# Transposed activations of a four-layer trunk: ACT reads a whole PSUM tile before DVE does

## The chip, the cores and the metric

The kernel runs on one core of one Trainium2 chip. The metric is the device time in microseconds (us) of one launch, as the median of several runs. PE is the matrix engine (TensorE), PEld its weight loads, DVE the vector engine, ACT the scalar engine, POOL is GpSimd and SP is SyncE, which here issues most DMAs.

## What is computed

A decoder trunk of four layers over 512 tokens of width 1024, in float32. Each layer normalises its input, mixes along the tokens with one of three mixers (S5, HGRN2, sliding-window attention, then S5 again), multiplies by a gate, projects back, normalises and adds:

```python
h = x
for i in range(DEPTH):                       # 4: S5, HGRN2, attention, S5
    u = rms_norm(h, norm_pre[i])
    if kind == 0:   y = s5_branch(u, ...)
    elif kind == 1: y = hgrn2_branch(u, ...)
    else:           y = swa_branch(u, ...)
    h = h + rms_norm(y, norm_post[i])
```

Each branch starts with a projection `u @ w_in` (1024 to between 2048 and 4096 columns). That first projection needs u with the channels on the partitions, so u is transposed.

## The kernel before

**Split products.** A float32 product is made of three matmuls on values that are rounded for the fast float32 path: every matrix is a high part and a low part (the rest). For the weights ACT copies the high part `whi` (w_conv, L182) and DVE subtracts for the low part `wlo` (L183). For the activations the high part is `xh`, the low part `xl`. In the weight-times-x loop (ws_steps, L228) each block of 128 channels k takes hi·xh, hi·xl and lo·xh in turn, so PE needs `xl` of a block one matmul after `xh` of it.

**From a layer to the next.** `out_proj` (L328) forms the output of layer L in PSUM tiles `ops` (L243) for four blocks of 128 tokens, tb 0 to 3. For each piece ACT squares it into `junk` for the sum of squares (L339) and DVE multiplies it by the gain into `yg` (L341). When a token block is complete, `finish` sums the two parts on DVE (`po_st`, L345), POOL raises to the power -1/2 (`rstd`, L253 and L254, giving `rs_r`), and DVE adds to the residual `h` (L350). `norm_stats` then prepares the next layer's input: ACT squares h (L274), POOL makes the factor, DVE scales (`xs`, L277). `spill` writes h to memory from SP (L356).

**The transposes.** `norm_xt` (L279 to L299) is called for token blocks (0, 1) together, for (2,) and for (3,). PE transposes blocks of xs into a PSUM tile `xtp` (L292). A tile has `per` slices, one slice per channel block k. For tokens (0, 1) it has two slices of 256 tokens, so there are four tiles; for (2,) and (3,) it has four slices of 128 tokens, so there are two tiles each. All these tiles, and some others of the mixers, share the tag "ca", of which there are two buffers: a third tile can be written only when the first has been read to its end. For every slice ACT scales and rounds it into `xh` (L296) and DVE forms scale times slice minus xh, which is `xl` (L298). The first layer has no low part of x there (`xl` is None); the three later entries do.

**Where they stand in the order.** The tiles of tokens (0, 1) are made inside the `out_proj` of the layer before, between the matmuls of token blocks 2 and 3. The tiles of (2,) and (3,) are made in the next layer's first projection (`first_blocks`, L301, for layers 1 and 2; the same pattern in `s5_rest` for layer 3, with the calls in its loop over half and b). There PE multiplies four blocks of output channels b by the first 256 tokens (half 0). Ahead of its fourth block PE transposes the two tiles of tb 2, named A and B here, then does the fourth block, then transposes the two tiles of tb 3, C and D here, and then starts half 1 (tokens 256 to 511), whose first matmul needs the first slice of C. C goes into A's buffer and D into B's.

```python
for half in range(2):
    for b in range(4):
        if half == 0 and b == 3:
            for _ in self.norm_xt(L, (2,)):       # tiles A, B
                pass
        self.ws(pss[b][...], w[b // 2], b % 2, self.x, half * 256, half * 256 + 256)
    if half == 0:
        for _ in self.norm_xt(L, (3,)):           # tiles C, D
            pass
```

In layers 1 and 2 the framework's scheduler puts the instructions of the engines in order, by its own estimates; layer 3 (L995ff) runs under a hand-written order for PE, DVE, ACT and SP, in which instructions stay as the code issues them. Beside the transposes, DVE and ACT have other work at each entry: in layer 1 the softmax of the lower bounds (`lb_e` and so on, L1060 to L1073, with one exp on ACT, L1062) and small tables of the later S5 layer (`lam`, `th`, `ap`, L404 to L479); in layer 2 the sine and cosine of the rotary embedding (L413 to L421, L1291); in layer 3 the S5 kernel tables (`q`, `vt`, `t`, L713 to L731), which wait for a parameter transfer `prm` (L706).

Of the kernel before, what the change touches and what calls it, by code (L numbers as in the profile page):

```python
# [20 lines left out]
KB = 8  # L21
# [87 lines left out]
class Trunk:  # L109
# [169 lines left out]
    def norm_xt(self, L, tbs):  # L279

        nc = self.nc
        xh, xl = self.x
        xs = self.xs
        n = len(tbs)
        c = slice(tbs[0] * 128, tbs[0] * 128 + 128 * n)
        per = 4 // n
        for k2 in range(KB // per):
            ps = self.psum.tile([P, per, 128 * n], F32, tag="ca", name="xtp", bufs=2)
            for kk in range(per):
                k = per * k2 + kk  # L290
                for i, tb in enumerate(tbs):
                    nc.tensor.transpose(ps[:, kk, i * 128:(i + 1) * 128], xs[:, tb, k * 128:(k + 1) * 128], self.ident)  # L292
            for kk in range(per):
                k = per * k2 + kk
                g = self.gpre[:, L * KB + k:L * KB + k + 1]
                nc.scalar.activation(out=xh[:, k, c], in_=ps[:, kk, :], func=AF.Copy, scale=g)  # L296
                if xl is not None:
                    nc.vector.scalar_tensor_tensor(out=xl[:, k, c], in0=ps[:, kk, :], scalar=g, in1=xh[:, k, c].bitcast(F32), op0=ALU.mult, op1=ALU.subtract)  # L298
            yield  # L299

# [1341 lines left out]
```

## Time and profile before

| | |
|---|---|
| median of 3 runs | 1119.49 us (1118.13 to 1121.62) |
| the profiled execution's own time | 1116.3 us |
| its span, first to last instruction | 1114.5 us |
| mean granted TensorE clock | 0.973 of full |
| PE, DVE, ACT, POOL busy | 93%, 67%, 45%, 9% of the span |
| chain that ended last | PE 63%, DVE 15%, ACT 6%, DMA 6%, issue 5% |

The profiled execution is 3.2 us below the median of the runs. Times of rows are microseconds from the start of the span. In a timeline a row is the start, the duration, the engine, line, operation, output <- inputs, shapes and count; in square brackets stands how long the engine was idle before and what ended the idle time. The second of two instructions of one engine often starts before the first has ended (by some tenths), so durations of neighbours can't be added; where that matters, the distance between starts is used. The granted clock of a stretch is a fraction of 2.4 GHz; at 0.50 PE runs at 1.2 GHz.

### The profile page before, as it was taken

What the parts mean: (1) busy time and instruction counts of PE and PEld (TensorE: products, weight loads), DVE (VectorE), ACT (ScalarE), POOL (GpSimd) and SP (SyncE); (2) the same over time, 40 slices, a digit from 0 to 9 for tenths busy, and PEclk for the clock granted to TensorE, in tenths of its full rate; (3) what the DMA queues carried; (4) which work ended last, traced back from release to release, by engine and by line L of the source; (5) the groups of instructions that cost most, each with busy time, mean ns of one, the idle gap of its engine ahead of it and who ended that gap; (6) DMA issues with size and microseconds to landing.
All of it is one profiled execution on the core that took longest, in us unless ns stands there. A gap on an engine that the chain in (4) does not pass through costs nothing.

```text
span 1114.5 us, 17031 instructions
## 1 busy us (share of the span) xinstructions
PE 1031.2 (93%) x6480; PEld 822.3 (74%) x6480; DVE 750.5 (67%) x1458; ACT 504.2 (45%) x933; POOL 103.2 (9%) x162
## 2 busy tenths in 40 slices
PE   5999975999999999999999898999997879988997
PEld 4755544778899798998978885666676767766876
DVE  6786759585698777887856565556664468863752
ACT  4344425554452314333244534688743355645540
POOL 2000000030200000000011022100002010100200
PEclk9999988999999999999999999999999889998999
DMA  6574233533432324414153452211125357544331
GB/s 230 137 190 126 74 85 98 171 114 126 143 103 81 114 71 132 144 65 151 61 189 124 122 145 62 74 57 53 61 95 167 117 155 238 173 124 146 104 103 57
DMA packets 70577, 133.31 MB, mean 120 GB/s; under 512 B 28896, under 2 KB 40032, under 8 KB 69472
## 3 DMA queue, kind: packets, MB, share of 16 engines
q1 hardware_dynamic: 65664, 119.04, 34.6%
q10 hardware_dynamic: 4832, 13.19, 3.6%
q8 instruction: 51, 0.84, 0.3%
q14 instruction: 30, 0.25, 0.1%
HBM read 100.51 MB, written 20.15 MB: 108 GB/s over the span
## 4 chain that ended last, share of the span: by engine, by line
PE 63%; DVE 15%; ACT 6%; DMA 6%; issue 5%; SPq 2%; POOL 1%; ACTq 1%; DVEq 0%; POOLq 0%
PE pj L228 26%; PE ops L243 13%; PE zps L243 4%; PE vps L243 3%; PE sps L1120 2%; PE scps L1328 2%; DVE wlo L183 2%; SPq L773 2%; ACT whi L182 2%; PE aops L1364 2%; DMA rsw<-rraw 1%; DMA prm<-in_s_bc 1%; PE ptp L1359 1%; DVE sg L1049 1%; PE yps L858 1%
## 5 line engine op out<-in xcount | busy, mean ns | idle before, releaser
L183 DVE TENSOR_TENSOR wlo<-wraw,whi 128x1024 fp32r<-128x1024 f32 x116 | 143.2, 1251 | 65.0 <-ACT whi L182 56.1
L228 PE MATMUL pj<-xh,whi 128*128 128x512 f32 (+1 forms) x496 | 182.3, 370 | 0.0
L228 PE MATMUL pj<-xl,whi 128*128 128x512 f32 (+1 forms) x496 | 177.9, 360 | 2.5 <-DVE xl L298 2.4
L228 PE MATMUL pj<-xh,wlo 128*128 128x512 f32 (+1 forms) x496 | 177.4, 359 | 0.0
L182 ACT ACTIVATE whi<-wraw 128x1024 fp32r<-128x1024 f32 x116 | 120.7, 1056 | 79.4 <-PE pj L228 38.2
L228 PE MATMUL pj<-xf,wraw 128*128 128x512 f32 (+1 forms) x320 | 116.0, 512 | 0.0
L228 PEld LDWEIGHTS pj<-xh,whi 128*128 128x128 f32 x496 | 96.3, 195 | 16.8 <-issue 5.8
L228 PEld LDWEIGHTS pj<-xl,whi 128*128 128x128 f32 x496 | 96.9, 196 | 14.6 <-DVE xl L298 3.2
L228 PEld LDWEIGHTS pj<-xh,wlo 128*128 128x128 f32 x496 | 96.5, 195 | 13.6 <-issue 1.7
L243 PE MATMUL ops<-whi,gh 128*128 128x512 f32 x256 | 101.6, 398 | 2.7 <-ACT gh L1051 2.2
L243 PE MATMUL ops<-wlo,gh 128*128 128x512 f32 x256 | 100.7, 394 | 1.1 <-DVE wlo L183 1.0
L243 PE MATMUL ops<-whi,gl 128*128 128x512 f32 x256 | 100.5, 395 | 0.0
L228 PEld LDWEIGHTS pj<-xf,wraw 128*128 128x128 f32 x320 | 59.2, 192 | 40.4 <-issue 36.7
L243 PEld LDWEIGHTS ops<-whi,gh 128*128 128x128 f32 x256 | 48.2, 188 | 13.8 <-ACT gh L1051 3.0
L243 PEld LDWEIGHTS ops<-wlo,gh 128*128 128x128 f32 x256 | 48.2, 188 | 13.2 <-DVE wlo L183 2.7
L243 PEld LDWEIGHTS ops<-whi,gl 128*128 128x128 f32 x256 | 48.1, 188 | 11.3 <-DVE gl L1052 0.9
L228 PE MATMUL pj<-yl,whi 128*128 128x512 f32 x128 | 51.0, 399 | 3.5 <-DVE yl L950 3.5
L228 PE MATMUL pj<-yh,whi 128*128 128x512 f32 x128 | 51.3, 401 | 0.5 <-ACT yh L946 0.5
L228 PE MATMUL pj<-yh,wlo 128*128 128x512 f32 x128 | 50.8, 397 | 0.0
L341 DVE TENSOR_TENSOR yg<-ops,gpost 128x512 f32<-128x512 f32 x32 | 21.9, 688 | 36.9 <-ACT junk L339 36.6
L243 PE MATMUL vps<-wlo,xh 128*128 128x256 f32 x160 | 45.3, 283 | 0.0
L243 PE MATMUL vps<-whi,xl 128*128 128x256 f32 x160 | 45.3, 283 | 0.0
(279 smaller groups left out, 2106.4 us busy)
## 6 DMA issues: line engine op xcount, KB each, us to landing
wraw<-in_s_in SPq DMA_DIRECT2D x32, 512.0 KB, 6.3
wraw<-in_hg_in SPq DMA_DIRECT2D x32, 512.0 KB, 3.6
wraw<-in_at_in SPq DMA_DIRECT2D x20, 512.0 KB, 4.2
wraw<-in_s_glu SPq DMA_DIRECT2D x16, 512.0 KB, 3.8
wraw<-in_s_out SPq DMA_DIRECT2D x16, 512.0 KB, 3.5
hd<-h SPq DMA_DIRECT2D x6, 1024.0 KB, 4.0
prm<-in_s_bc SPq DMA_DIRECT2D x16, 256.0 KB, 4.6
ub<-ut SPq DMA_DIRECT2D x16, 256.0 KB, 4.2
```

What stands on the lines that cost most here:

```text
L182: nc.scalar.activation(out=hi, in_=raw, func=AF.Copy)
L183: nc.vector.tensor_tensor(out=lo, in0=raw, in1=hi.bitcast(F32), op=ALU.subtract)
L228: self.nc.tensor.matmul(ps, lhsT=l[k // 4][:, k % 4, c], rhs=r[:, k, n0:n1], start=k == 0 and n == 0, stop=k == KB - 1 and n == len(terms) ...
L243: self.nc.tensor.matmul(ps, lhsT=l[:, k, c], rhs=r[k // per][:, k % per, :], start=k == 0 and n == 0, stop=k == KB - 1 and n == 2)
L341: nc.vector.tensor_tensor(out=yg[:, tb, f], in0=ps, in1=gp[:, f], op=ALU.mult)
L773: nc.sync.dma_start(out=toep[128 - n:128, jj, :, :], in_=ksb[0:n].rearrange("p a g h -> p (a g) h"))
L858: nc.tensor.matmul(o, lhsT=u[:, g, :], rhs=d["toep"][:, :, g, :], start=True, stop=False)
L1049: nc.vector.tensor_tensor(out=sg, in0=sg, in1=y[:, k, :], op=ALU.mult)
L1120: nc.tensor.matmul(ps[:, c, :], lhsT=k[:, c * 128:c * 128 + 128], rhs=q4[:, c, :, 1, :], start=True, stop=True)
L1328: nc.tensor.matmul(ps[:, bb, lo:256], lhsT=self.q[r, 4 * p + 2 * b2 + bb, qs], rhs=self.k[r, p, ks], start=True, stop=True)
L1359: nc.tensor.transpose(tp[:, f, bb, :], sm[:, bb, f * 128:f * 128 + 128], self.ident)
L1364: nc.tensor.matmul(ops[64 * i:64 * i + 64].rearrange("p b q -> p (b q)"), lhsT=self.v[:, n - 1 + f, kv * 64:kv * 64 + 64], rhs=pts[i][:, f ...
```

## The change

In `norm_xt` the loop over the slices of a tile is split in two: ACT's reads of all slices come first, then DVE's reads of all slices. The same instructions run with the same operands, only the order in which they are issued is another.

```diff
             for kk in range(per):
                 k = per * k2 + kk
                 g = self.gpre[:, L * KB + k:L * KB + k + 1]
                 nc.scalar.activation(out=xh[:, k, c], in_=ps[:, kk, :], func=AF.Copy, scale=g)
-                if xl is not None:
+            if xl is not None:
+
+                for kk in range(per):
+                    k = per * k2 + kk
+                    g = self.gpre[:, L * KB + k:L * KB + k + 1]
                     nc.vector.scalar_tensor_tensor(out=xl[:, k, c], in0=ps[:, kk, :], scalar=g, in1=xh[:, k, c].bitcast(F32), op0=ALU.mult, op1=ALU.subtract)
             yield
```

Lines behind L299 are four lower down in the changed kernel (L339 becomes L343, and so on), and the xl line moves from L298 to L302.

**ACT at the entry of layer 1**, from the exp of the lower bounds on (tiles xtp_2454 and xtp_2467 are A and B). Before:

```order
L1062 ACTIVATE lb_e_2328<-lb_e_2328 128x32 [waits DVE_49]
L509 DMA lam_2765<-in_s5_lam 128x288 [waits DMAHW4_49,DMAHW0_49,Activation_49]
L296 ACTIVATE xh_2125<-xtp_2454,gpre_96 128x128 [waits PE_49]
L296 ACTIVATE xh_2125<-xtp_2467,gpre_96 128x128 [waits PE_49]
L296 ACTIVATE xh_2125<-xtp_2454,gpre_96 128x128 [waits DVE_49]
L296 ACTIVATE xh_2125<-xtp_2467,gpre_96 128x128 [waits DVE_49]
L431 ACTIVATE lam_2765<-lam_2765 128x96 [waits DMAHW0_49]
```

and with the change:

```order
L1066 ACTIVATE lb_e_2328<-lb_e_2328 128x32 [waits DVE_49]
L513 DMA lam_2765<-in_s5_lam 128x288 [waits DMAHW4_49,DMAHW0_49,Activation_49]
L296 ACTIVATE xh_2125<-xtp_2454,gpre_96 128x128 [waits PE_49]
L296 ACTIVATE xh_2125<-xtp_2454,gpre_96 128x128 x3
L296 ACTIVATE xh_2125<-xtp_2467,gpre_96 128x128 [waits PE_49]
L296 ACTIVATE xh_2125<-xtp_2467,gpre_96 128x128 x3
L435 ACTIVATE lam_2765<-lam_2765 128x96 [waits DMAHW0_49]
```

Before, every read of ACT but a tile's first waits for DVE, and the two tiles take turns; now only the first of a tile waits, for PE, and the tiles come one after the other. The entries of layers 2 and 3 change in the same way.

**DVE in the out_proj of layer 0**, where the tiles of tokens (0, 1) for layer 1 are read (xtp_2249 and xtp_2288 are the third and fourth of them). Before:

```order
L341 TENSOR_TENSOR yg_1971<-ops_2215,gpost_1969 128x512 [waits Activation_49]
L298 SCALAR_TENSOR_TENSOR xl_2126<-xtp_2249,gpre_96,xh_2125 128x256 [waits Activation_49]
L345 TENSOR_REDUCE po_st_2261<-po_ss_1974 128x1
L350 SCALAR_TENSOR_TENSOR h_1747<-yg_1971,rs_r_2264,h_1747 128x1024 [waits DVE_49,Pool_49]
L298 SCALAR_TENSOR_TENSOR xl_2126<-xtp_2249,gpre_96,xh_2125 128x256 [waits Activation_49]
L277 TENSOR_SCALAR xs_2127<-h_1747,rs_r_2271 128x1024 [waits Activation_49,Pool_49]
L298 SCALAR_TENSOR_TENSOR xl_2126<-xtp_2288,gpre_96,xh_2125 128x256 [waits Activation_49] x2
L341 TENSOR_TENSOR yg_1971<-ops_2275,gpost_1969 128x512 [waits Activation_49]
```

and with the change:

```order
L345 TENSOR_TENSOR yg_1971<-ops_2215,gpost_1969 128x512 [waits Activation_49]
L349 TENSOR_REDUCE po_st_2261<-po_ss_1974 128x1
L302 SCALAR_TENSOR_TENSOR xl_2126<-xtp_2249,gpre_96,xh_2125 128x256 [waits PE_49,Activation_49]
L302 SCALAR_TENSOR_TENSOR xl_2126<-xtp_2249,gpre_96,xh_2125 128x256
L354 SCALAR_TENSOR_TENSOR h_1747<-yg_1971,rs_r_2264,h_1747 128x1024 [waits DVE_49,Pool_49]
L277 TENSOR_SCALAR xs_2127<-h_1747,rs_r_2271 128x1024 [waits Activation_49,Pool_49]
L302 SCALAR_TENSOR_TENSOR xl_2126<-xtp_2288,gpre_96,xh_2125 128x256 [waits PE_49,Activation_49]
L302 SCALAR_TENSOR_TENSOR xl_2126<-xtp_2288,gpre_96,xh_2125 128x256
L345 TENSOR_TENSOR yg_1971<-ops_2275,gpost_1969 128x512 [waits Activation_49]
```

`po_st` moves ahead of both low parts of the third tile, and both of them ahead of `h`; in the fourth tile the second low part no longer waits for ACT.

**DVE in layer 1 after the transposes**, around the first two `wlo` there (sin_2794 and cos_2795 are ACT's table values for the later S5 layer). Before:

```order
L446 TENSOR_TENSOR ap_2806<-mag_2791,cos_2795 128x64 [waits Activation_49]
L462 SCALAR_TENSOR_TENSOR u1_2842<-ap_2806,lam_2765 128x64 [waits DVE_49]
L404 TENSOR_TENSOR pw1_2873<-ap_2806 128x128
L464 TENSOR_TENSOR u1_2842<-u1_2842,u2_2843 128x64 [waits DVE_49]
L404 TENSOR_TENSOR pw2_2874<-ap_2806 128x128
L465 TENSOR_TENSOR co_2841<-u1_2842,den_2844 128x64 [waits DVE_49]
L467 TENSOR_TENSOR u2_2843<-ap_2806,lam_2765 128x64
L466 SCALAR_TENSOR_TENSOR u1_2842<-ap_2806,lam_2765 128x64 [waits DVE_49]
L472 TENSOR_SCALAR co_2841<-co_2841,cst_94 128x64
L468 TENSOR_TENSOR u1_2842<-u1_2842,u2_2843 128x64 [waits DVE_49]
L406 TENSOR_TENSOR ap_2806<-pw1_2873,pw2_2874 128x64
L183 TENSOR_TENSOR wlo_2367<-wraw_2362,whi_2366 128x1024 [waits PE_49,Activation_49]
```

and with the change:

```order
L467 TENSOR_TENSOR u2_2843<-ap_2806,lam_2765 128x64 [waits DVE_49]
L183 TENSOR_TENSOR wlo_2367<-wraw_2362,whi_2366 128x1024 [waits PE_49,Activation_49]
L183 TENSOR_TENSOR wlo_2371<-wraw_2364,whi_2370 128x1024 [waits DMAHW1_49,PE_49,Activation_49]
L450 TENSOR_TENSOR ap_2806<-mag_2791,cos_2795 128x64 [waits Activation_49]
L466 SCALAR_TENSOR_TENSOR u1_2842<-ap_2806,lam_2765 128x64 [waits DVE_49]
L408 TENSOR_TENSOR pw1_2873<-ap_2806 128x128
```

The eleven small table instructions that stood ahead of the first `wlo` now stand behind the second, since ACT's cosine for them has moved behind two weight copies and two evacuations.

## Rows read from the trace of the kernel before

**Rows 1.** The page's busy times: us, share of the span, instructions.
```profile
PE 1031.2 (93%) x6480; PEld 822.3 (74%) x6480; DVE 750.5 (67%) x1458; ACT 504.2 (45%) x933; POOL 103.2 (9%) x162
```
**Rows 2.** Waits by engine and releaser: us in total, times, longest us.
```profile
ACT xh L296 <- DVE xl L298: 23.8, 25, 3.6
...
PE xtp L292 <- DVE xl L298: 12.3, 4, 4.9
```
**Rows 3.** Timeline of ACT, out_proj of layer 0 and entry of layer 1.
```profile
292.69 0.47 ACT L296 ACTIVATE xh<-xtp,gpre 128x256 fp32r<-128x256 f32 x1 [1.76 <-DVE xl L298]
...
301.59 0.23 ACT L1062 ACTIVATE lb_e<-lb_e 128x32 f32<-128x32 f32 x1 [1.57 <-DVE lb_e L1061]
...
302.05 0.62 ACT L296 ACTIVATE xh<-xtp,gpre 128x128 fp32r<-128x128 f32 x2 [0.23 <-ACT lb_e L1062]
```
**Rows 4.** Timeline of DVE, the same stretch.
```profile
286.62 0.48 DVE L298 SCALAR_TENSOR_TENSOR xl<-xtp,gpre,xh 128x256 fp32r<-128x256 f32 x1
287.01 0.15 DVE L345 TENSOR_REDUCE po_st<-po_ss 128x1 f32<-128x2 f32 x1
...
292.17 0.48 DVE L298 SCALAR_TENSOR_TENSOR xl<-xtp,gpre,xh 128x256 fp32r<-128x256 f32 x1
...
293.77 0.69 DVE L341 TENSOR_TENSOR yg<-ops,gpost 128x512 f32<-128x512 f32 x1
...
303.05 0.60 DVE L298 SCALAR_TENSOR_TENSOR xl<-xtp,gpre,xh 128x128 fp32r<-128x128 f32 x2
...
306.40 0.21 DVE L436 TENSOR_TENSOR lrdt<-lam 128x64 f32<-128x64 f32 x1
...
307.80 0.25 DVE L298 SCALAR_TENSOR_TENSOR xl<-xtp,gpre,xh 128x128 fp32r<-128x128 f32 x1
```
**Rows 5.** Timeline of PE, entry of layer 1, and a wait later in that layer.
```profile
306.54 1.26 PE L292 MATMUL xtp<-cst,xs 128*128 128x128 f32 x8 [2.59 <-DVE xl L298]
...
308.68 0.41 PE L228 MATMUL pj<-xl,whi 128*128 128x256 f32 x1
...
336.23 1.05 PE L1107 MATMUL dps<-hq,hk 128*128 128x192 f32 x5 [1.00 <-DVE st L1110]
```
**Rows 6.** Windows: us, then busy of PE, PEld, DVE, ACT, POOL; PEclk, DMA, GB/s.
```profile
304.00:312.00 8.00, 5.46 (x32) 5.18 (x33) 6.70 (x31) 6.10 (x17) 0.00 (x0) 0.79 0.01 2
330.00:340.00 10.00, 8.99 (x70) 8.82 (x70) 9.83 (x42) 2.60 (x3) 0.00 (x0) 1.00 0.42 136
```
**Rows 7.** Timelines of ACT, DVE and PE, entry of layer 2.
```profile
619.72 0.61 ACT L296 ACTIVATE xh<-xtp,gpre 128x128 fp32r<-128x128 f32 x2
...
620.65 0.60 DVE L298 SCALAR_TENSOR_TENSOR xl<-xtp,gpre,xh 128x128 fp32r<-128x128 f32 x2
...
623.41 1.09 PE L292 MATMUL xtp<-cst,xs 128*128 128x128 f32 x8 [3.37 <-DVE xl L298]
...
625.23 0.42 PE L228 MATMUL pj<-xl,whi 128*128 128x256 f32 x1
```
**Rows 8.** Timelines of ACT, DVE and PE, entry of layer 3 and a later wait.
```profile
856.43 0.40 ACT L718 ACTIVATE c<-prm,cst 128x128 f32<-128x128 f32 x1 [4.58 <-DMA prm<-in_s_bc]
...
857.92 1.22 DVE L727 TENSOR_TENSOR vt<-ap,q 128x1024 f32<-128x1024 f32 x1
...
859.85 0.35 DVE L298 SCALAR_TENSOR_TENSOR xl<-xtp,gpre,xh 128x128 fp32r<-128x128 f32 x1 [0.43 <-ACT xh L296]
...
861.83 1.11 PE L292 MATMUL xtp<-cst,xs 128*128 128x128 f32 x4 [4.87 <-DVE xl L298]
...
864.30 1.22 DVE L730 TENSOR_TENSOR t<-ap,q 128x1024 f32<-128x1024 f32 x1
...
867.14 0.34 DVE L298 SCALAR_TENSOR_TENSOR xl<-xtp,gpre,xh 128x128 fp32r<-128x128 f32 x1
...
867.54 0.58 PE L228 MATMUL pj<-xl,whi 128*128 128x256 f32 x1 [1.76 <-DVE xl L298]
...
894.61 0.42 DVE L713 TENSOR_TENSOR q<-prm,co 128x256 f32<-128x256 f32 x1 [10.79 <-DMA prm<-in_s_bc]
```

## The prediction, made before the changed kernel had run

> **What bounds the kernel now.** I read the page's busy times first [rows 1]: PE is busy for 93% of the span, DVE for 67%, ACT for 45%. The end can only come earlier where PE stands still or runs slowly. The waits by engine and releaser come next [rows 2]: ACT's high parts waited 25 times for DVE's low parts, 23.8 us in all, and PE waited 12.3 us in four pieces to write a transposed tile, since the buffer was still being read by DVE. The first number is large and mostly worth nothing, as ACT has time. The second is PE's own idle time. Three of its four pieces stand in the timelines: 2.59 us at the entry of layer 1 [rows 5], 3.37 at layer 2 [rows 7], 4.87 at layer 3 [rows 8]; the fourth, 1.5, follows at layer 3. So the change is worth what it does at three entries, and at each I ask two things: when does DVE finish tiles A and B, which frees the buffers for C and D, and when does the first low part of C exist, which PE needs to go on.
>
> **Price of the pieces.** One low part takes 0.35 us [rows 8], two back to back 0.60 [rows 4, 7], so a further one costs 0.25 and four about 1.1. Two high parts take 0.62 [rows 3], so four also come to about 1.1. Turn by turn with nothing else between, one slice takes 0.35 plus a wait of 0.43 [rows 8], some 0.79, thus eight slices 6.3 us against about 2 × 1.1 us for DVE alone.
>
> **Term 1: the chain of statistics ahead of each entry, 1.2 us earlier.** In out_proj ACT's second read of the fourth tile of tokens (0, 1) waited 1.76 us for DVE [rows 3]. DVE's low part (start 292.17 [rows 4]) had stood behind xs, and ACT's junk, which must come before DVE's yg, stood behind that read. With the change ACT has both high parts done long before. DVE then runs two low parts and yg without a gap. Low part to next instruction is 0.39 (286.62 to 287.01 [rows 4]). Moreover po_st goes ahead of the third tile's low part, so that h, the squares and xs of token block 2 start 0.39 earlier, while both low parts run in the time that POOL takes for its power. So yg comes at 292.17 - 0.39 + 2 × 0.39 = 292.56 instead of 293.77 [rows 4]: 1.2 us. Everything behind it (h, the last squares, xs of block 3, and the small DMAs that ACT and SP issue after them) moves by this. The same pattern precedes layers 2 and 3, where ACT's longest wait is 3.6 [rows 2]. By itself it gives PE nothing, since the first transposes of an entry wait for no one; its worth lies in the next terms.
>
> **Term 2: layer 1, 2.8 us.** ACT's exp ended at about 301.8 [rows 3], now 300.6. High parts of A take until 301.8, of B until 302.9. DVE's lower bounds were done at 303.05, when its low parts started [rows 4]; now 301.85, and all highs of A are there. Low parts of A last until 303.0, of B until 304.1. PE's fourth block ended at 306.54 - 2.59 = 303.95 [rows 5], so the 2.59 are gone: C is transposed at once, D with a few tenths of a wait. What is late next is DVE. The order puts ten small table instructions ahead of C's low parts. Six such, a reciprocal among them, took from 306.40 to 307.80 [rows 4], so ten cost 1.9 to 2.3, from 304.1 to about 306.2. PE's matmul comes 0.4 after its low part starts (867.14 to 867.54 [rows 8]): 306.4 to 306.8 against 308.68 [rows 5]. That is 1.9 to 2.3. A second part is the clock: it was granted at 0.79 between 304 and 312, with PE busy for 5.46 us [rows 6], of which 0.21 × 5.46 = 1.1 us were lost. The wait that is left is about 1 to 1.5 us; one of 1.00 at 336.23 [rows 5] lies in a stretch with the clock at 1.00 [rows 6]. Bounds 1.9 and 3.4; I take 2.8, nearer that row.
>
> **Term 3: layer 2, 2.8 us.** High parts of A started at 619.72 and low parts at 620.65 [rows 7]; by term 1 ACT starts at 618.5 and is through with A at 619.65, and DVE, free at 619.45, does A's low parts until 620.9. ACT's cosine, which stood between the high parts, comes behind B. C is transposed at 620.95 instead of 623.41, its highs start at 621.6 and its first low part at 622.8, so PE goes on at 623.2 instead of 625.23 [rows 7]: 2.0. With a clock part like layer 1's 1.1 it is 3.1. I take 2.8.
>
> **Term 4: layer 3, 4.6 us.** Here the order is written by hand and the turns are strict. ACT's c waited for the parameter transfer until 856.43 [rows 8]; with term 1 that is 855.2. ACT's highs of A and B are then ready at 857.8, while DVE still does vt (857.92, 1.22 long, now from 856.72). A's low parts end at 859.05, B's at 860.15. C is transposed at 859.05 against 861.83, and t starts at 860.1 against 864.30. From t to the first low part of C there are 2.84 us (to 867.14), and 0.4 to PE's matmul: 863.3 against 867.54 [rows 8], 4.25 earlier. The next blocks no longer follow DVE and ACT's pitch of 0.79, which I put at 0.3. If the parameter transfer does not move, 3.4 is left.
>
> **Term 5: DVE in layer 1, charged 0.7.** Eleven table instructions that DVE did while ACT made weight copies now stand behind two wlo. One is 0.21 long [rows 4], so DVE stands idle for about 2.2 there and does this work later, in front of the heads. Bounds: 0, if PE has other matmuls to fill with, and 2.2. DVE is busy for 9.83 of 10 us later in the layer, but PE's wait in that stretch is only 1.00 [rows 5, 6]; I take a third.
>
> Nothing else changes: no instruction is added, each is as long as before, the DMAs stay in their order on SP and POOL. Work of ACT and DVE that moves earlier in tokens (0, 1) is under matmuls.
>
> **Sum.** 2.8 + 2.8 + 4.6 - 0.7 = 9.5. Against the profiled execution, 1116.3, that is 1106.8; the median of the runs is 3.2 higher, and on it the forecast is 1119.5 - 9.5 = **1110.0 us**. With the terms' bounds the gain lies between 1.9 + 2.0 + 3.4 - 2.2 = 5.1 and 3.4 + 3.1 + 4.6 = 11.1, 1114.4 to 1108.4. A median of three moves by another 1 to 2 (the runs went from 1118.1 to 1121.6), so I go down to 1106.
>
> **Rivals.** *Layer 3's gain is taken back at a parameter transfer.* DVE waited 10.79 us until 894.61 for a later prm [rows 8]. If that transfer is held by the weight loads ahead of it and not by PE's progress, what PE wins before is lost there, and 4.9 is left: 1114.6. For it: the wait is the longest of its kind in this stretch. Against: the loads ahead of it need buffers that PE frees, so it should move with PE. **0.20.**
>
> *Finer turns are better.* Reading a whole tile first makes its first low part come three high parts later, 3 × 0.25 = 0.75, at each tile for which PE waits with nothing else to do: C of each layer. In layers 1 and 2 both engines already had a second tile to work on while they waited, so there the total of their work is unchanged and only this cost remains. Layer 3 keeps the gain from its strict turns, about 3.1. Net 3.1 - 2 × 0.75 = 1.6: 1118.0, within the resolution. The Trainium skill ("Perfetto Trace Analysis", Optimizing Scalar/DVE Operations) speaks for this side: where the scalar and vector engines are not saturated but cause bubbles on others, breaking work into smaller pieces may let it finish sooner. By that rule turns are the finer pieces, and the engines are unsaturated here (45% and 67%); by the rows above the bubble comes from the end of a tile, not from its first slice. **0.12.**
>
> *Slower: DVE becomes the bound of layer 1's first heads.* The scheduler's new order leaves DVE idle for 2.2 us and puts up to 17 small instructions of 0.2, 3.4 in all, ahead of the heads' hk and hqt. If no matmuls of the projection are left to cover it, PE waits 5.6 for each of the first two head pairs, 11.2, in a stretch where DVE is already busy 98% [rows 6]. Layer 1's gain is lost with it: 11.2 - 2.8 - 4.6 = 3.8 slower, 1123.3. It decides from the point at which the wait of 1.00 at 336.23 [rows 5] grows beyond what the entries give. **0.05.**
>
> That the change does nothing is excluded: the order shows ACT's reads free of waits for DVE.
>
> **How the numbers follow.** A measurement of this kernel tells 0.3%, 3.4 us, from no change. The forecast's case has 0.63 and spans 1106 to 1114; with the first rival (1114.6, plus some run to run) the range is 1106.0 to 1116.5 and leaves out the other two, 0.17, and a little below. Both first cases are faster by over 3.4 us (below 1116.1): 0.83. The second rival is the same: 0.12. The third is slower: 0.05.
>
> **What would show it.** ACT's wait for DVE in the list of waits should nearly vanish, and PE's 12.3 us for xtp shrink to 3 to 4, most of it at layer 3. yg after the fourth tile should start about 1.2 earlier relative to its transposes. The clock around the entries of layers 1 and 2 should stay near 1. In layer 3, t should start about 4 us earlier relative to PE's last matmul of half 0. I am wrong if PE's low-part wait at C grows by what xtp's shrinks, if the DVE wait near the first heads of layer 1 grows to several us, or if the wait for prm at 894.61 grows by 4.

## The result, and the profile after

The changed kernel took 1108.03 us (median of 4 runs, 1105.03 to 1110.78) against 1119.28 (4 runs, 1118.13 to 1121.62): a ratio of 0.9896, 95% interval 0.9865 to 0.9927, 11.2 us less, where 9.5 were forecast. Run again later beside other kernels it took 1105.91 (6 runs) against 1119.78 (11 runs): 0.9871 (0.9841 to 0.9901).

The two profiled executions differ by less, 1110.78 against 1116.3 us, 5.5 us: the profile before came from an execution 3 us below the median of its kernel, the profile after from the slowest of its four. Where that comes from is shown below: a transfer landed late in layer 3, and the clock was lower behind it. The change is not the cause.

The page's first part after the change, as [rows 1]:

```profile
PE 1029.4 (93%) x6480; PEld 821.3 (74%) x6480; DVE 747.7 (67%) x1458; ACT 500.4 (45%) x933; POOL 103.9 (9%) x162
```

DVE and ACT are busy for about as long as before. Of the 5.5 us between the two spans 3.7 are idle time of PE (83.3 before, 79.6 after); the other 1.8 are busy time of PE (1031.2 and 1029.4), since the same matmuls run at a higher granted clock in some stretches. The waits by engine and releaser show the first part, beside [rows 2]:

```profile
ACT xh L296 <- PE xtp L292: 5.1, 6, 2.0
...
PE xtp L292 <- DVE xl L302: 4.4, 3, 3.1
...
PE pj L228 <- DVE xl L302: 3.2, 3, 1.9
```

ACT's high parts wait for PE's transposes now, and no wait of theirs for DVE is among the hundred largest. PE's wait to write a transposed tile is 4.4 instead of 12.3, a little above the forecast of 3 to 4; two waits at layer 3, 3.12 and 0.38, are most of it. PE's wait for low parts grew from 2.4 to 3.2, far less than the other shrank.

**Layer 1.** DVE's timeline after the change, as [rows 4]:

```profile
291.70 0.87 DVE L302 SCALAR_TENSOR_TENSOR xl<-xtp,gpre,xh 128x256 fp32r<-128x256 f32 x2
292.48 0.68 DVE L345 TENSOR_TENSOR yg<-ops,gpost 128x512 f32<-128x512 f32 x1
...
301.95 2.16 DVE L302 SCALAR_TENSOR_TENSOR xl<-xtp,gpre,xh 128x128 fp32r<-128x128 f32 x8
305.02 0.26 DVE L439 TENSOR_TENSOR th<-lam 128x96 f32<-128x96 f32 x1 [0.90 <-ACT lam L435]
...
306.77 2.06 DVE L302 SCALAR_TENSOR_TENSOR xl<-xtp,gpre,xh 128x128 fp32r<-128x128 f32 x8
```

yg comes at 292.48 instead of 293.77. PE was 0.09 ahead there, so the chain of statistics is 1.20 earlier: term 1 to the hundredth. The eight low parts of A and B take 2.16 us in one go. But the table instructions then start 0.9 late, since ACT's lam waited for its transfer. ACT and PE in the same stretch, as [rows 3, 5]:

```profile
300.78 2.18 ACT L296 ACTIVATE xh<-xtp,gpre 128x128 fp32r<-128x128 f32 x8 [0.23 <-PE xtp L292]
304.70 0.28 ACT L435 ACTIVATE lam<-lam 128x96 f32<-128x96 f32 x1 [1.75 <-DMA lam<-in_s_lam]
```

```profile
303.71 1.12 PE L292 MATMUL xtp<-cst,xs 128*128 128x128 f32 x8
305.29 0.74 PE L228 MATMUL pj<-xh,whi 128*128 128x256 f32 x4 [0.47 <-ACT xh L296]
307.08 0.38 PE L228 MATMUL pj<-xl,whi 128*128 128x256 f32 x1 [1.05 <-DVE xl L302]
```

C and D are transposed without a wait (2.59 before). PE's first low part of C is at 307.08 against 308.68, 1.5 earlier when the 0.09 are taken off. What is missing to the forecast's 1.9 to 2.3 is less than DVE's wait of 0.90 for lam. When the change was run again, lam had landed by 302.66, and PE's wait for the low part was 0.56 instead of 1.05.

**Layer 3.** DVE's timeline, as [rows 8]:

```profile
855.21 2.15 DVE L302 SCALAR_TENSOR_TENSOR xl<-xtp,gpre,xh 128x128 fp32r<-128x128 f32 x8
857.27 1.22 DVE L734 TENSOR_TENSOR t<-ap,q 128x1024 f32<-128x1024 f32 x1
...
859.67 2.15 DVE L302 SCALAR_TENSOR_TENSOR xl<-xtp,gpre,xh 128x128 fp32r<-128x128 f32 x8
```

Layer 3 began 2.68 us earlier in this execution. Taking that off, t starts 864.30 - 857.27 - 2.68 = 4.35 earlier (4.2 forecast), the first low part of C 867.14 - 859.67 - 2.68 = 4.8 (4.3 forecast).

### The profile page after: what moved, and what is told of

Its sections match the earlier page's. It is cut to its first block, busy times and chain, and to the rows that moved or that the text cites. A ratio compares the mean times of both kernels' runs of the same rounds, so it can differ in the third digit from the quotient of the medians.

```text
span 1109.0 us, 17044 instructions
## 1 busy us (share of the span) xinstructions
PE 1029.4 (93%) x6480; PEld 821.3 (74%) x6480; DVE 747.7 (67%) x1458; ACT 500.4 (45%) x933; POOL 103.9 (9%) x162
## 4 chain that ended last, share of the span: by engine, by line
PE 64%; DVE 13%; DMA 7%; ACT 6%; issue 5%; SPq 2%; POOL 1%; ACTq 1%; DVEq 0%; POOLq 0%
PE pj L228 26%; PE ops L243 14%; PE zps L243 4%; PE vps L243 3%; PE scps L1332 3%; PE sps L1124 2%; DVE wlo L183 2%; SPq L777 2%; PE aops L1368 2%; ACT whi L182 2%; DMA prm<-in_s_bc 1%; DMA rsw<-rraw 1%; PE yps L864 1%; PE ptp L1363 1%; PE yps L862 1%
```

## Stage by stage, over all the traces

Runs of one kernel scatter by 3 to 11 us, so that medians tell parts of 2 us apart only roughly. The traces do better for some stages: layer 1's rest, for example, lies between 239.7 and 239.8 us in seven of them. Others scatter in one and the same program, as layer 2's rest does (152.5 and 150.0 with the change). For each layer I took from PE's timeline the start of its first projection (the first matmul after the last `ops`), C's first low part, and the first `ops` of its own out_proj. **Entry** is from the first to 60 matmuls after the second, **rest** from there to the third. **Late** is one stretch of 120 matmuls in layer 3 (it starts at 973.7 in the trace before), and **prm** the time from SP's issue of the last parameter transfer to the DVE instruction q that reads it. All in us; bold where the layer has the whole reads.

| kernel (whole reads in) | L1 entry | L1 rest | L2 entry | L2 rest | L3 entry | late | prm |
|---|---|---|---|---|---|---|---|
| before (none) | 25.4 | 240.7 | 26.3 | 150.3 | 33.8 | 14.7 | 6.9 |
| layer 1 | **22.1** | **239.7** | 27.0 | 150.4 | 33.7 | 18.5 | 9.0 |
| layer 2 | 23.9 | 241.4 | **23.5** | **151.4** | 32.7 | 18.4 | 8.4 |
| layers 1, 2 | **22.9** | **239.8** | **24.7** | **150.9** | 33.5 | 15.2 | 7.3 |
| layer 3 | 24.9 | 242.2 | 26.2 | 152.3 | **28.0** | 18.4 | 8.1 |
| the change | **23.0** | **239.7** | **24.7** | **152.5** | **28.2** | 20.8 | 10.6 |
| the change again | **22.0** | **239.8** | **23.4** | **150.0** | **27.4** | 14.9 | 7.0 |
| out_proj tiles only | 23.7 | 241.3 | 23.7 | 149.7 | 31.2 | 19.1 | 9.0 |
| entry tiles only | 23.2 | 239.8 | 26.2 | 150.2 | 28.6 | 18.1 | 8.0 |
| C and D by turns | 21.6 | 242.1 | 22.9 | 150.4 | 27.7 | 18.6 | 8.9 |
| pairs | 22.6 | 239.7 | 23.0 | 150.2 | 29.1 | 19.3 | 9.5 |
| layer 2 pairs, else whole | **22.8** | **239.8** | 23.1 | 152.2 | **27.6** | 16.4 | 7.2 |

Means of bold against those of the kernels that read that whole layer by turns (the first, and the runs on other layers): layer 1's entry 22.6 against 24.7, its rest 239.8 against 241.4; layer 2's entry 24.0 against 26.5, its rest 151.2 against 151.0; layer 3's entry 27.8 against 33.4. In sum -2.2 - 1.7 - 2.5 + 0.2 - 5.7 = -11.8, beside -11.2 and -13.9 by the medians. Apart from late, a stage of one program differs by up to 2.5 us between two executions (layer 2's rest), so I take single parts as known to about 1 us, an estimate.

## The experiments

All edits but the last two, the pairs, are shown against the changed kernel and put the turns back where a condition holds; those of the pairs are shown against the kernel before.

**Out_proj tiles only, entry tiles only.** For the first:

```diff
                 nc.scalar.activation(out=xh[:, k, c], in_=ps[:, kk, :], func=AF.Copy, scale=g)
-            if xl is not None:
-
+                if xl is not None and n == 1:
+                    nc.vector.scalar_tensor_tensor(out=xl[:, k, c], in0=ps[:, kk, :], scalar=g, in1=xh[:, k, c].bitcast(F32), op0=ALU.mult, op1=ALU.subtract)
+            if xl is not None and not (n == 1):
                 for kk in range(per):
```

> Only the two-slice tiles of tokens (0, 1) are read whole; the four-slice tiles of the entries keep their turns. Theory of separate terms: yg after the fourth tile comes 1.2 us earlier relative to the transposes in all three out_projs, and each entry starts its low parts up to 1.2 earlier, less what small DMAs hold back: about 3 us in all, 1116.3 (1115 to 1118). Rival, the whole gain comes from the four-slice tiles and the earlier statistics are hidden: 1119.3 as before. Rival, the statistics chain is most of the gain: below 1113.

For the second the condition is the other one:

```diff
-                if xl is not None and n == 1:
+                if xl is not None and n == 2:
...
-            if xl is not None and not (n == 1):
+            if xl is not None and not (n == 2):
```

> Only the four-slice tiles at the entries of the layers are read whole; the out_proj keeps its turns. Theory of separate terms: what the whole change gives (11.2 us) without about 3 for the statistics chain: 1111 (1110 to 1113). Rival, the statistics chain is hidden: 1108 as with the whole change. Rival, the chain is most: above 1114.

Measured: 1110.96 us, ratio 0.9928 (0.9902 to 0.9954), and 1110.56, 0.9914 (0.9893 to 0.9936), against 1119.23. So they save 8.3 and 8.7 us alone and 11.2 together: the second agrees with the expectation, the first with its rival, and the parts overlap. The table says where. In layer 2 the out_proj tiles alone shorten the entry by 2.8 (23.7 against 26.5), more than the whole change, and the entry tiles alone by 0.3; in layer 3 they give 2.2 and 4.8 of the 5.7. I had counted an earlier start as at most 1.2 per entry, and that held: against the trace before, C's first low part with the out_proj tiles alone comes 0.85, 1.24 and 1.24 us earlier, counted from the start of layers 1, 2 and 3, which is 3.3 in all. What comes on top is PE's clock. In the 60 matmuls behind that low part it was granted at 1.00, 1.00 and 0.77, and before at 0.86, 0.82 and 0.64; they took 7.2, 7.2 and 7.8 us instead of 8.2, 8.6 and 9.2, another 3.6 in all. With the entry tiles alone it was 1.00, 0.81 and 0.77. How much of this the edit did is open, since the clock there differs in kernels that read an entry in the same way: with layer 1 read by turns, a wait of 2.46 at C's transposes left the 60 matmuls at 1.00 (run on layer 2 below), and one of 1.98 was followed by 0.83 (run on layer 3).

**By layer.** The condition was `L != 3`, `L == 3`, `L != 1` and `L != 2` in these four, for example:

```diff
-                if xl is not None and n == 1:
+                if xl is not None and L != 3:
...
-            if xl is not None and not (n == 1):
+            if xl is not None and not (L != 3):
```

> The change in layer 3's input alone (its out_proj tiles and its four-slice tiles). Theory of separate terms: 4.6 by the prediction, 5.7 by the shift of the matmuls between the two traces (1.0 in the out_proj, 4.65 at the entry): 1113.6 to 1114.7. Rival, a later parameter transfer takes it back: 1118 to 1119. Layers 1 and 2 should have stages as long as before within 0.3.

> The change in the inputs of layers 1 and 2 alone. Theory of separate terms: the complement of the run on layer 3, 11.2 - 5.7 = 5.5 at most; by the traces 3.3 in layer 1 and 1.6 at the entry of layer 2: 1114.4. Rival, layer 2 gives its part back at the rotary embedding's transfers, as the one profile of the changed kernel shows (2.2 lost after 1.6 won): 1116.5, with layer 2 as long as before or longer in this run's trace too.

> The change in layer 1's input alone. By the traces so far layer 1 (from its first projection to its out_proj) is 3.8 us shorter with the change: 1115.4. By the prediction's terms it is 2.8 - 0.7 = 2.1: 1117.1. Rival, the new order of layer 1 costs DVE time: 1119 or more, and PE's stage after the entry longer than before.

> The change in layer 2's input alone. By the prediction 2.8: 1116.4. By the difference of the runs of layers 1 and 2 together and the traces of layer 1, 3.7: 1115.5. Rival, given back at the rotary embedding's transfers: 1118.5 to 1119.3, with layer 2 as long as before in its trace.

Measured: layer 3 alone 1115.22, 0.9955 (0.9933 to 0.9977), 4.0 us less than 1119.23; layers 1 and 2 1111.72, 0.9928 (0.9901 to 0.9956), 7.5 less. Later, against 1118.58: layer 1 alone 1115.32, 0.9961 (0.9940 to 0.9983), 3.3 less; layer 2 alone 1115.51, 0.9971 (0.9950 to 0.9992), 3.1 less. The layers add: 4.0 + 7.5 = 11.5, and 3.3 + 3.1 = 6.4 of the 7.5. Layers 1 and 2 together saved more than the 5.5 that I had as the most; layer 3 alone lies 0.5 above its expected range. There layers 1 and 2, which read by turns as before, were 1.0 and 2.0 longer than in the trace before and not equal within 0.3: this is the scatter of the table. No layer gives its part back, so both rivals of giving back fall, and so does the one that expected layer 1 to be slower.

What looked like giving back in the profiles is the column "late". PE's wait there in the trace before and in the one after, each with DVE's q ahead of it, first before:

```profile
970.44 0.43 DVE L713 TENSOR_TENSOR q<-prm,co 128x256 f32<-128x256 f32 x1 [1.49 <-DMA prm<-in_s_bc]
...
976.24 0.44 PE L860 MATMUL yps<-w,spre 128*64 128x128 f32 x4 [0.22 <-DVE spre L845]
```

then after:

```profile
963.51 0.42 DVE L717 TENSOR_TENSOR q<-prm,co 128x256 f32<-128x256 f32 x1 [5.19 <-DMA prm<-in_s_bc]
...
969.31 0.70 PE L864 MATMUL yps<-w,spre 128*64 128x128 f32 x4 [2.82 <-DVE spre L849]
```

The last parameter transfer took 6.9 us until q in one and 10.6 in the other; spre and two weight low parts stand behind q on DVE, and the stretch took 14.7 and 20.8 us. The two stretches as windows (us; busy time of PE, PEld, DVE, ACT, POOL; granted clock; DMA share; GB/s), before and after:

```profile
973.70:988.40 14.70, 12.13 (x128) 9.29 (x124) 10.99 (x15) 8.23 (x14) 0.40 (x1) 1.00 0.56 167
963.05:983.80 20.75, 14.96 (x127) 11.75 (x124) 13.72 (x18) 8.83 (x15) 1.56 (x3) 0.75 0.44 125
```

So only 3.2 of the 6.0 are idle time of PE; the other 2.8 are longer busy time at a clock of 0.75. In all the traces the clock was 1.00 where the stretch took 14.7 to 15.2, and 0.75 to 0.91 where it took more. Taking these 6.0 off, the two profiles are 11.5 apart, and the medians 11.2. The runs on layer 1 and layer 2 alone, where layer 3 is as before, have 18.5 and 18.4 there.

**The change once more**, without an edit, to settle this:

> The whole change once more on the same chip as the version above. Theory, the profile of the changed kernel was a slow one of its runs because the last parameter transfer landed after 10.6 us: the stage of layer 3 behind it (20.8 us there, 14.7 before, 18.1 to 19.3 in most experiments, whether or not layer 3 is changed) comes out between 18 and 19.5 and the median at 1108. Rival, the change itself lengthens that stage: 20.5 or more again.

Measured: 1105.91 us, and 14.9 in that stretch with the transfer at 7.0. So the change does not lengthen it. My expected 18 to 19.5 and 1108 missed too: this transfer scatters between 6.9 and 10.6 us over the traces, 7.0 and 10.6 in one and the same program, and why it does was not tried.

**C and D by turns:**

```diff
-                if xl is not None and n == 1:
+                if xl is not None and tbs[0] == 3:
...
-            if xl is not None and not (n == 1):
+            if xl is not None and not (tbs[0] == 3):
```

> Tiles C and D (tokens of block 3) go back to turns slice by slice, all others are read whole. Theory of the two ends: whole reads pay at A and B, since their end frees the buffers, and cost at C, since PE waits for its first low part; so C's transposes come as early as with the whole change, the first low part follows after 1.7 us instead of 3.2 to 3.4 in layers 1 and 2, in layer 3 nothing changes (DVE's tables set it): 2.5 to 3 us faster than the whole change, about 1105.5. Rival, whole reads are better at every tile: 1109 to 1111, and the first blocks of half 1 follow the turns' pitch of 0.79.

Measured: 1108.30, 0.9900 (0.9874 to 0.9926), the whole change's time and 2.8 above the expectation. The entries are as the theory has them: from C's transposes to its first low part 1.9 and 2.2 us in layers 1 and 2 (3.4 and 3.2 in the trace after), and the entries 1.0 and 1.2 shorter than the means with whole reads. But layer 1's rest is 242.1 instead of 239.8: the scheduler had put layer 1 into another order for this code, and PE was idle there for 0.9 us more, at gl (below) above all, and busy for 1.4 us more, since the clock fell behind that wait. This takes the gain.

**What layer 1's rest is made of.** It is 239.7 to 239.8 in every kernel with the entry tiles of layer 1 whole or in pairs, and 240.7 to 242.2 in every other. Two thirds of the difference of the means, 1.1 of 1.7 us, appear at one wait. PE and DVE before, around it:

```profile
379.81 0.65 PE L1187 MATMUL gps<-cst,hog 128*128 128x128 f32 x4 [2.27 <-DVE gl L1192]
```

```profile
375.54 1.22 DVE L183 TENSOR_TENSOR wlo<-wraw,whi 128x1024 fp32r<-128x1024 f32 x1
376.67 0.69 DVE L550 TENSOR_TENSOR rt<-e 128x512 f32<-128x512 f32 x1
377.27 0.68 DVE L552 TENSOR_TENSOR rot<-rot,rt 128x512 f32<-128x512 f32 x1
377.88 1.22 DVE L183 TENSOR_TENSOR wlo<-wraw,whi 128x1024 fp32r<-128x1024 f32 x1
379.01 0.74 DVE L1192 SCALAR_TENSOR_TENSOR gl<-gps,gn,gh 128x512 fp32r<-128x512 f32 x1
```

and after:

```profile
377.24 0.66 PE L1191 MATMUL gps<-cst,hog 128*128 128x128 f32 x4 [1.17 <-DVE gl L1196]
```

```profile
374.17 2.35 DVE L183 TENSOR_TENSOR wlo<-wraw,whi 128x1024 fp32r<-128x1024 f32 x2
376.44 0.74 DVE L1196 SCALAR_TENSOR_TENSOR gl<-gps,gn,gh 128x512 fp32r<-128x512 f32 x1
377.10 1.28 DVE L554 TENSOR_TENSOR rt<-e 128x512 f32<-128x512 f32 x2
```

Before, two table instructions for layer 3 (rt, rot) stood between the weight copies, ahead of gl, for which PE waited 2.27; now they stand behind gl, and the wait is 1.17. It is 1.15 to 1.20 in all seven traces with 239.7 to 239.8 and 2.27 to 2.34 in the five others. Most of the rest of the 1.7 is the clock behind the longer wait, which fell in two of the five: in the run on layer 3 and with C and D by turns. The 4 us from the gps of the shown wait before, and from the same gps with C and D by turns:

```profile
379.81:383.81 4.00, 4.00 (x20) 3.39 (x21) 1.45 (x3) 1.29 (x2) 0.00 (x0) 1.00 0.87 273
375.44:379.44 4.00, 4.00 (x13) 3.35 (x14) 3.10 (x5) 0.69 (x1) 0.00 (x0) 0.58 0.41 131
```

PE did 13 matmuls there instead of 20. So the new order of layer 1 is worth 0.9 us between the two traces before and after, and 1.7 in the mean, with two falls of the clock in it. DVE did stand idle ahead of the first weight low part, as I had read it, but the wait of PE near the first heads that I had feared for (1.00 at 336.23 [rows 5]) is 1.30 in the trace after, no more:

```profile
312.42 1.23 DVE L183 TENSOR_TENSOR wlo<-wraw,whi 128x1024 fp32r<-128x1024 f32 x1 [2.10 <-ACT whi L182]
333.08 0.89 PE L1111 MATMUL dps<-hq,hk 128*128 128x192 f32 x4 [1.30 <-DVE st L1114]
```

**Pairs:**

```diff
-            for kk in range(per):
-                k = per * k2 + kk
-                g = self.gpre[:, L * KB + k:L * KB + k + 1]
-                nc.scalar.activation(out=xh[:, k, c], in_=ps[:, kk, :], func=AF.Copy, scale=g)
...
+            for k0 in range(0, per, 2):
+                ks = [per * k2 + kk for kk in range(k0, k0 + 2)]
+                g = {k: self.gpre[:, L * KB + k:L * KB + k + 1] for k in ks}
+                for k in ks:
+                    nc.scalar.activation(out=xh[:, k, c], in_=ps[:, k % per, :], func=AF.Copy, scale=g[k])
+                if xl is not None:
+                    for k in ks:
+                        nc.vector.scalar_tensor_tensor(out=xl[:, k, c], in0=ps[:, k % per, :], scalar=g[k], in1=xh[:, k, c].bitcast(F32), op0=ALU.mult, op1=ALU.subtract)
```

> The four-slice tiles are read in two pairs: ACT two slices, DVE two, ACT two, DVE two. Theory of the turns: each turn costs a wait; half of the turns in layer 3, so that its entry lies in the middle between before (33.8 us from the first projection to the 60th low part) and the whole change (28.2), and C's first low part comes 0.5 earlier than with whole reads in layers 1 and 2: 1108 to 1111. Rival, only the first wait counts and pairs already give all: at or below 1108.

Measured: 1107.57, 0.9901 (0.9871 to 0.9931), just below the expected range and on the rival's side. The two-slice tiles of tokens (0, 1) are one pair each, so they are read whole here. Layer 3's entry is 29.1: pairs give three quarters of the gain there and not half, but 2.2 of it are what the whole out_proj tiles gave alone. Of the three waits of ACT for DVE in a tile of four slices pairs leave one. In layers 1 and 2 C's first low part follows after 2.1 and 1.8 us, and layer 2's entry is 1.0 shorter than the mean with whole reads. About 0.6 of this is the clock: the two traces with whole reads and a clock of 1.00 have 23.4 and 23.5 there, the other two 24.7. The four us from C's first low part in layer 2, as windows (us; busy time of PE, PEld, DVE, ACT, POOL; granted clock; DMA share; GB/s), of the change:

```profile
620.80:624.80 4.00, 4.00 (x27) 4.00 (x27) 1.37 (x5) 1.10 (x5) 0.00 (x0) 0.74 0.00 0
```

of the run on layers 1 and 2:

```profile
619.58:623.58 4.00, 4.00 (x23) 4.00 (x23) 1.84 (x7) 0.95 (x4) 0.00 (x0) 0.62 0.02 6
```

of the change again:

```profile
619.23:623.23 4.00, 4.00 (x34) 4.00 (x34) 1.84 (x7) 1.65 (x5) 0.00 (x0) 1.00 0.02 5
```

and of pairs:

```profile
619.73:623.73 4.00, 4.00 (x34) 4.00 (x34) 1.85 (x7) 1.45 (x6) 0.00 (x0) 1.00 0.00 0
```

At a clock of 0.62 PE does 23 matmuls in the time of 34. In the trace before, the same windows have 0.72 at layer 1 and 0.61 at layer 2. With whole reads the clock came through layer 1 at 1.00 in all the traces, but through layer 2 only in two of four; the same program had both. PE's idle time before it, in the trace after:

```profile
617.62 0.66 PE L292 MATMUL xtp<-cst,xs 128*128 128x128 f32 x4 [0.86 <-DVE xl L302]
619.16 0.56 PE L228 MATMUL pj<-xh,whi 128*128 128x256 f32 x2 [0.88 <-ACT xh L296]
```

Two waits in place of the one of 3.37 [rows 7]. When the change was run again and the clock stayed at 1.00, it had the same two, 0.82 and 0.88. With pairs there is a single one of 1.42 ahead of C's transposes, with the out_proj tiles alone one of 2.26, and both had 1.00. What decides between the two levels is not shown.

**Pairs in layer 2, whole reads elsewhere:**

```diff
-            for k0 in range(0, per, 2):
-                ks = [per * k2 + kk for kk in range(k0, k0 + 2)]
+            w = 2 if L == 2 else per
+            for k0 in range(0, per, w):
+                ks = [per * k2 + kk for kk in range(k0, k0 + w)]
```

> Pairs in layer 2, whole reads in layers 1 and 3. By the traces layer 2 is 2.6 us shorter with pairs than with whole reads (173.2 against 175.9), and layer 3's entry 1.0 shorter with whole reads than with pairs: 2.6 faster than the whole change and 1 faster than pairs everywhere, 1105.5 if the whole change gives 1108. The clock granted in the 4 us from the first low part of layer 2 should be 1.00, where the whole change had 0.62 and 0.74. Rival, layer 2 is set by the rotary embedding's transfers later on: as the whole change within 1.

Measured: 1105.55, 0.9866 (0.9839 to 0.9892), beside 1105.91 for the change itself in the same comparison. The entry of layer 2 is 23.1, as meant, its clock 1.00 and its entry 0.9 below the mean with whole reads. Its rest was 152.2 in this trace, at the upper end of 149.7 to 152.5 that all kernels have. So no version here is measurably better than the change; the theory's 2.6 were worked out against three traces with whole reads in layer 2, in two of which the clock had fallen; half of the 2.6 stood in layer 2's rest, which scatters.

## Why the prediction was right

- **Term 1** (statistics 1.2 us earlier): 1.20 in the trace. What I said of its worth was too low, since I gave it none by itself: alone the out_proj tiles save 8.3 us by the medians. The earlier start is 0.85 to 1.24 per entry there, as counted; the same again came from the clock.
- **Term 2** (layer 1's entry, 2.8): 2.2. The buffers came free as worked out, and the clock stayed at 1.00. What is missing came for the most part from the transfer of lam, which I had let move with its issue: the entries are 22.0 and 22.1 in the two traces where lam did not hold ACT up and 22.8 to 23.0 in the three others.
- **Term 3** (layer 2's entry, 2.8): 2.5. C's transposes were 2.5 earlier, as forecast to a tenth. The first low part came only 1.15 earlier instead of 2.0 (625.23 to 620.80, less the 3.28 by which the layer began earlier). It followed C's transposes after 3.18 instead of 1.82, the price named in the second rival, and PE's clock fell in that execution and not when the change was run again.
- **Term 4** (layer 3's entry, 4.6): 5.7, the mechanism as written down: t 4.35 earlier, then the first low part, 4.8 earlier. The price of the turns was too high: eight slices took 5.3 us there (859.07 to 864.39) and not 6.3, since the first slice of a second tile does not wait.
- **Term 5** (layer 1's new order, a charge of 0.7) is the step that failed, by its sign: the new order gains 0.9 between the two traces and 1.7 in the mean. I had read where eleven instructions went in one place and priced their delay. DVE did stand idle there, 2.10 us until 312.42, but PE's wait near the first heads grew only by 0.3. The same new order took two other instructions off the path 70 us later, at gl, where PE's wait shrank by 1.1, and I had not read that place.
- **The sum** was 9.5 against 11.2 by the runs and 11.8 by the stages: the entries of layers 1 and 2 gave 0.6 and 0.3 less, that of layer 3 gave 1.1 more, and term 5 was off by 2.4. That the sum came near is in part luck: the misses have both signs, and the clock, which I had counted in layers 1 and 2 alone, made differences in layer 3 and behind gl too.
- **The first rival**, layer 3's gain lost at a later parameter transfer: the transfer read at 894.61 gave nothing back (read at 884.62 after a wait of 9.15 instead of 10.79), and a later one scatters without the change.
- **The second rival**, finer turns: its price is real and about what I had (0.75). In layers 1 and 2, over all traces, C's first low part follows its transposes after 2.4 to 3.4 us with whole reads (mean 2.9 of 11), after 1.7 to 2.6 with turns (mean 2.0 of 10). But the end of A and B decides more. The rule of the Trainium skill ("Perfetto Trace Analysis", Optimizing Scalar/DVE Operations) is on breaking up instructions, and none was broken up here. As far as finer turns stand for smaller pieces, the traces agree for the one tile whose first slice PE waits for (2.0 against 2.9), and not for the tiles whose end it waits for (12.3 us of waiting with turns, 4.4 without).
- **The third rival**: PE's wait there is 1.30, not 5.6.

## What to carry to other kernels

Where two engines read one buffer, first ask what is waited for behind it: the first piece or the release of the buffer. For the release, let each engine read all of it in one go: eight slices took 2.2 us per engine, against 5.3 in the strict turns of layer 3. And when a change makes a scheduler reorder a stage, compare that stage's length in several traces, since reading one place of the new order gave the wrong sign. With the length, compare the granted clock: a wait of PE was sometimes followed by several us at a lower clock, and differences of 1 to 3 us between two traces came from this here.

## What the runs showed of the hardware that was not expected

- One transfer scatters much between executions: the last parameter transfer was read 6.9 to 10.6 us after its issue, and the 120 matmuls of PE behind it took 14.7 to 20.8 us, a difference of half the size of the change. At the two ends the clock was 1.00 and 0.75.
- The granted clock of one program in one place was 0.74 in one execution and 1.00 in another, with the same two short waits of PE ahead of it (0.86 and 0.88, 0.82 and 0.88).
- In one execution a small transfer (lam) issued 1.3 us earlier was ready no earlier (304.70 against 304.78); in the next it was ready 2 us earlier.
